# Stick-breaking attention on one core: the values product in plain fp32, two heads side by side on TensorE's columns

## The chip, the core and the metric

The kernel runs on one core of one Trainium2 chip. The metric is device microseconds for one execution of the whole program, of which the runs give a median and a lowest and highest. A profile of one execution gives the span, from the first to the last instruction, and the times of every instruction. The engines are called PE (TensorE's matmuls), PEld (its weight loads), DVE (VectorE), ACT (ScalarE), POOL (GpSimd) and SP (SyncE, which starts most transfers here).

## What is computed

A two-layer trunk over 512 tokens of width 1024. Layer 0 mixes tokens by stick-breaking attention with 16 heads of width 64; layer 1 mixes them by a gated MLP. Each is followed by a SwiGLU feed-forward part. Only the attention is touched:

```python
for qb in range(S // SB_QBLOCK):          # 4 blocks of 128 queries
    z = einsum('bhtd,bhsd->bhts', q[..., q0:kend, :], k[..., :kend, :]) * scale
    log_beta = log_sigmoid(z)
    log_1m = where(before, log_sigmoid(-z), 0.0)
    later = cumsum(log_1m, reverse=True) - log_1m
    a = where(before, exp(log_beta + later), 0.0)
    out = einsum('bhts,bhsd->bhtd', a, v[..., :kend, :])
```

The weights `a` of one head are a 512 x 512 triangle of 128 x 128 blocks, ten of them not empty. The last line, weights times V, is what this document calls the values product.

## The kernel before, in words

**Products of split numbers.** Nearly every product is made of reduced fp32 numbers (type F32R). A number is split (`split`, line 89) into a high part, which ACT writes (line 93), and a low part, the rest, which DVE subtracts (line 94). `mm3` (line 81) then issues three matmuls into one accumulator: high by high, high by low, low by high.

**The attention's stages** (lines 655 to 875). The sixteen heads go by pairs, a pair being 128 rows of q, k or 128 columns of V.

- V (lines 551 to 570) is computed first, in two halves of 512 columns; `v_evac` splits each half into `Vh` and `Vl`, four ACT copies and four DVE subtractions per half. They live in slots of the pool `s4`, which has 28.
- `scores` (line 738) multiplies q and k for some blocks of a pair. A head uses 64 of the array's 128 rows, and the two heads are issued in turn into two PSUM banks `zb`. ACT takes the sigmoid (line 759), DVE runs a scan (line 764) and a difference (line 769), which leaves the weights in `ga`.
- `flip` (line 775) turns three or four 128 x 128 blocks of weights on PE (line 78) into the bank `tw` of that head, and splits them into the tile `ar`, high and low part side by side; `ar` has two buffers.
- `values` (line 789) takes the turned blocks as the moving operand and V as the stationary one. For each head it goes over two pieces; a piece is one block row of V by 128 or 256 columns, and takes the three matmuls of `mm3`. All 128 columns of the pair's V are loaded for either head, so each of the two banks `av` has 64 rows of use and 64 rows that nobody reads.
- `finish` (line 804) copies the useful half of each `av` bank into one tile `of` (two ACT copies, line 810) and splits that into `o`, which the output projection reads later.

**Order of the work.** In the attention PE's order is written out by hand: `pe["chain"]` ties every matmul to the one before it. Per pair there are three flips of either head, three calls of `scores` for the next pair, and three calls of `values` per head (`LATE`, `EARLY[0]`, `EARLY[1]`). Between them `fill` issues steps of other products: q and k of later pairs (bank `pqk`, lines 676 to 685), and in the end parts of the output projection (bank `y`). One step of q and k is three matmuls of 512 columns. The piece widths of one head are 128 and 256 for `LATE` and for `EARLY[0]`, and 256 and 256 for `EARLY[1]`.

A background job `Bg` (line 274) computes the modulation vectors meanwhile: SP loads 512 KB tiles `rawada`, DVE multiplies and adds them (line 268, `G`, `A`, `B`). DVE and ACT also split the weights that PE will need (`wh`, `wl`, lines 93 and 94). The order on DVE and ACT is made by the scheduler when the program is built, not by hand; it follows the program's order roughly. DVE works its queue in order.

Of the kernel before, what the change touches and what calls it, by code (L numbers as in the profile page):

```python
# [8 lines left out]
F32 = mybir.dt.float32  # L9
F32R = mybir.dt.float32r  # L10
AF = mybir.ActivationFunctionType
ALU = mybir.AluOpType

P = 128
T = 512
# [10 lines left out]
def trunk(ctx: ExitStack, tc: tile.TileContext, A: dict, out: bass.AP):  # L26
# [6 lines left out]
    npool = ctx.enter_context(tc.tile_pool(name="npool", bufs=2))  # L33
# [9 lines left out]
    def nm(s):  # L43
        uid[0] += 1
        return f"{s}_{uid[0]}"

    def slot(dt, name, a=2, b=512):
        return s4.tile([P, a, b], dt, tag="s4", name=nm(name))

    def bank(name, tag="b"):  # L50
        return psum.tile([P, 512], F32, tag=tag, bufs=6 if tag == "b" else 2, name=nm(name))

    dve, act = nc.vector, nc.scalar
    pe = {"prev": None, "chain": False}

    def pe_op(b):

        if pe["chain"] and pe["prev"] is not None:
            order(b, pe["prev"])
        pe["prev"] = b  # L60

    def order(b, before):
        tc.add_manual_dep(
            b.ins, before.ins.name,
            mybir.DependencyInfo(mybir.DependencyClass.NoSync, mybir.DependencyReason.DATA),
            reason="order",
        )

    def mm(o, l, r, start, stop, after=None):
        b = nc.tensor.matmul(o, l, r, start=start, stop=stop, skip_group_check=True)  # L70
        pe_op(b)
        if after is not None:
            order(b, after)
# [3 lines left out]
    def transpose(o, i):  # L77
        last_tp[0] = nc.tensor.transpose(o, i, ident)  # L78
        pe_op(last_tp[0])

    def mm3(o, lh, ll, rh, rl, start, stop):
        mm(o, lh, rh, start, False)
        mm(o, lh, rl, False, False)
        mm(o, ll, rh, False, stop)
# [4 lines left out]
    def split(hi, lo, src, hi_dve=False):  # L89
        if hi_dve:  # L90
            dve.tensor_copy(hi, src)
        else:
            act.activation(hi, src, AF.Copy)  # L93
        dve.tensor_tensor(lo, src, hi.bitcast(F32), ALU.subtract)  # L94
# [453 lines left out]

    hT = new_hT()

    Vh = [[slot(F32R, "Vh") for _ in range(2)] for _ in range(2)]
    Vl = [[slot(F32R, "Vl") for _ in range(2)] for _ in range(2)]

    def v_step(vb, hf, k, w):
        for part in range(2):
# [11 lines left out]

    def v_evac(vb, hf):
        for tt in range(NT):
            split(Vh[hf][tt // 2][:, tt % 2, :], Vl[hf][tt // 2][:, tt % 2, :], vb[tt][:])  # L570

    onec = oneb[:, 0:1]

# [8 lines left out]
    def cols0(acc, n):  # L582

        ps = bank("ab0", "p")
        for i in range(n):
            mm(ps[:, i : i + 1], acc[:, i * P : (i + 1) * P], onec, True, True)
        return ps
# [31 lines left out]
    vb = [bank("v0") for _ in range(NT)]  # L619
# [7 lines left out]
    for b in range(1, 4):  # L627
# [7 lines left out]
        ps = cols0(acc, 4)  # L635
# [16 lines left out]
    fwork["raw"] = ctx.enter_context(tc.tile_pool(name="wraw2", bufs=2))  # L652
    v_evac(vb, 0)
    o8 = []
    with tc.tile_pool(name="att", bufs=1) as att, tc.tile_pool(name="att2", bufs=2) as att2:

        qk = {}

# [48 lines left out]
        def fill(n, at=None):  # L707
            for j in range(n):
                next(fgen, None)
                if j == at:  # L710
                    bg.step(1)
# [9 lines left out]
        def attend(i):  # L721

            weights = {}
            vc = slice(i % 4 * P, (i % 4 + 1) * P)
            vhf = i // 4

            def layout(js):
                offs, N = {}, 0
                for j in js:
                    offs[j] = N
                    N += T - P * j
                return offs, N

            def scores(js):

                q, kt = qk[i]  # L740
                offs, N = layout(js)
                for j in js:
                    o, n = offs[j], T - P * j
                    js_ = slice(j * P, (j + 1) * P)
                    for t, (a, b) in enumerate(((0, 0), (0, 1), (1, 0))):
                        for h in range(2):
                            r = slice(64 * h, 64 * h + 64)
                            mm(
                                zb[h][:, o : o + n], q[r, a, js_], kt[r, b, j * P : T],
                                j == js[0] and t == 0, t == 2,  # L750
                            )
                wide = js[0] != 2
                g = att.tile(
                    [P, 2, T + 4 if wide else 260], F32, tag=f"ga{wide}",
                    bufs=3 if wide else 1, name=nm("ga"),
                )
                with tc.issue_after(table.ins):
                    for h in range(2):
                        last_act[0] = act.activation(g[:, h, :N], zb[h][:, :N], AF.Sigmoid, scale=-1.0)

                for h in range(2):
                    for e, j in enumerate(js):
                        o, n = offs[j], T - P * j
                        dve.tensor_tensor_scan(  # L764
                            left[:, h, o + 1 : o + e + 1 + n], g[:, h, o - e : o + n],
                            tri[:, 1 - e : n + 1], 1.0, ALU.mult, ALU.max,
                        )
                M = N + len(js) - 1
                dve.tensor_tensor(g[:, :, :M], left[:, :, :M], left[:, :, 1 : M + 1], ALU.subtract)
                for e, j in enumerate(js):  # L770
                    weights[j] = (g, offs[j] + e)

            turned = {}

            def flip(blocks, h):

                ps = tw[h]
                n = 0
                for jj, js in blocks:
                    for j in js:  # L780
                        g, o = weights[j]
                        o += (jj - j) * P
                        transpose(ps[:, n : n + P], g[:, h, o : o + P])
                        n += P
                ar = att2.tile([P, 2, T], F32R, tag="ar", name=nm("ar"))
                split(ar[:, 0, :n], ar[:, 1, :n], ps[:, :n])
                turned[blocks[0][0], h] = ar

            def values(blocks, h, stop):

                ar = turned[blocks[0][0], h]
                start = blocks is LATE
                n = 0
                for jj, js in blocks:
                    w = len(js) * P
                    mm3(
                        av[h][:, js[0] * P : js[0] * P + w],
                        Vh[vhf][jj // 2][:, jj % 2, vc], Vl[vhf][jj // 2][:, jj % 2, vc],
                        ar[:, 0, n : n + w], ar[:, 1, n : n + w],
                        start and n == 0, stop and jj == 3,  # L800
                    )
                    n += w

            def finish():
                o = slot(F32R, "o")
                o8.append(o)
                f = npool.tile([P, 512], F32, tag="n", name=nm("of"))
                for h in range(2):
                    r = slice(64 * h, 64 * h + 64)
                    act.activation(f[r, :], av[h][r, :], AF.Copy)  # L810
                split(o[:, 0, :], o[:, 1, :], f[:])

            return scores, flip, values, finish

# [6 lines left out]
        LATE = ((2, (2,)), (3, (2, 3)))  # L821
        EARLY = ((0, (0,)), (1, (0, 1))), ((2, (0, 1)), (3, (0, 1)))
        vb = [bank("v1") for _ in range(NT)]
# [9 lines left out]
            bg.step(1)  # L833
        v_evac(vb, 1)
        tw = [bank("tw") for _ in range(2)]
        av = [bank("av") for _ in range(2)]
        fill(3, 1)
        cur[0](B0)
        for n in FIRST:
# [1 line left out]
        for i in range(NPAIR):  # L841
            scores, flip, values, finish = cur
            more = i + 1 < NPAIR
            F = iter(FILLS if i < 6 else LAST[i - 6])
            flip(LATE, 0)
            flip(LATE, 1)
            fill(next(F))
            if more:
                cur = attend(i + 1)
                cur[0](B31)  # L850
            fill(next(F), 1)
            values(LATE, 0, False)
            values(LATE, 1, False)
            fill(next(F))
            flip(EARLY[0], 0)
            flip(EARLY[0], 1)
            fill(next(F), 1)
            if more:
                cur[0](B2)
            fill(next(F), 1)  # L860
            values(EARLY[0], 0, False)
            values(EARLY[0], 1, False)
            flip(EARLY[1], 0)
            flip(EARLY[1], 1)
            fill(next(F))
            if more:
                cur[0](B0)
            fill(next(F), 1)
            values(EARLY[1], 0, True)
            values(EARLY[1], 1, True)  # L870
            finish()
        for _ in fgen:
            pass
# [361 lines left out]
```

## Time and profile before

| | before |
|---|---|
| time, median of 3 runs | 1181.23 us |
| lowest and highest | 1174.74 and 1182.79 us |
| span of the profiled execution | 1176.5 us |
| PE, PEld busy | 97%, 86% of the span |
| DVE, ACT busy | 75%, 47% of the span |
| mean granted TensorE clock | 0.990 |
| matmuls of the values product (`av`) | 288, from 112.0 to 268.4 us |

For the profiled execution the span is what is given; its own time is not listed apart from the three runs. The three runs lie within 0.7% of each other.

How to read it: a matmul's recorded time contains the way through the array, and matmuls overlap, so a sum of recorded times is more than the time that they take. What one matmul costs in a row of them is the distance from its start to the next start. In a timeline, the first column is the start, the second the time from the first start to the last end of a merged group, and brackets give idle time of the engine before it and who ended it. In the table of windows each engine has its busy time and, in brackets, the count of its instructions.

### The profile page before, as it was taken

Reading aid. Unit: us, or ns where it says so; the run is one execution under the profiler, and the core shown is the slowest. Engines: PE = TensorE matmul, PEld = TensorE weight load, DVE = VectorE, ACT = ScalarE, POOL = GpSimd, SP = SyncE. Lnnn points to the kernel's source line nnn. Section 1 sums busy time; section 2 is a strip of 40 time slices with the busy share of each in tenths; the row PEclk is TensorE's granted clock in tenths of the full one; section 3 lists DMA queues with packets and bytes.
Section 4 is the critical chain, followed back from the end, with each engine's and each line's share of the span. In section 5 each row is a group of like instructions: output and inputs, shape, how many; then the busy total and the mean of one; then the engine's idle time right before and its main releaser. Section 6 shows DMA issues by size and latency. Waiting matters only on the chain.

```text
span 1176.5 us, 18192 instructions
## 1 busy us (share of the span) xinstructions
PE 1140.3 (97%) x7296; PEld 1011.7 (86%) x7296; DVE 884.8 (75%) x1171; ACT 557.8 (47%) x935; POOL 20.2 (2%) x35
## 2 busy tenths in 40 slices
PE   5999999999999999999999999999999999999997
PEld 4776778888999999998878887988999999988886
DVE  6888998875998988878686864668889898873213
ACT  6444444554665555563143633526555555572112
POOL 0100000000000000000000100001000000000000
PEclk8999999999999999999999999999999999999999
DMA  8666452113424444338886473324244544244211
GB/s 328 201 213 231 144 161 72 55 54 126 160 92 144 134 139 142 122 112 262 281 286 237 151 250 125 109 71 156 80 143 126 161 127 142 75 127 160 90 54 72
DMA packets 48777, 173.93 MB, mean 148 GB/s; under 512 B 5674, under 2 KB 6058, under 8 KB 48692
## 3 DMA queue, kind: packets, MB, share of 16 engines
q1 hardware_dynamic: 46964, 166.48, 43.7%
q0 software_dynamic: 1728, 6.29, 1.4%
q8 instruction: 57, 0.93, 0.3%
q14 instruction: 28, 0.23, 0.1%
HBM read 164.36 MB, written 8.39 MB: 147 GB/s over the span
## 4 chain that ended last, share of the span: by engine, by line
PE 73%; DVE 11%; DMA 10%; ACT 3%; issue 3%; SPq 0%; DVEq 0%; ACTq 0%
PE r L70 31%; PE y L70 20%; DMA rawada<-in_ada 5%; PE v L70 4%; PE pqk L70 4%; PE gu L70 4%; DVE wl L94 2%; PE av L70 2%; PE u L70 2%; DVE left L764 1%; PE z L70 1%; DVE B L268 1%; DMA raw<-in_wdown 1%; PE tw L78 1%; DMA raw<-in_win_v 1%
## 5 line engine op out<-in xcount | busy, mean ns | idle before, releaser
L70 PE MATMUL y<-wh,as 128*128 128x512 f32 x832 | 264.0, 395 | 0.4 <-ACT gu L964 0.4
L93 ACT ACTIVATE wh<-raw 128x1024 fp32r<-128x1024 f32 x112 | 118.3, 1060 | 215.4 <-PE y L70 102.7
L94 DVE TENSOR_TENSOR wl<-raw,wh 128x1024 fp32r<-128x1024 f32 x112 | 136.3, 1221 | 107.4 <-ACT wh L93 107.1
L70 PEld LDWEIGHTS y<-wh,as 128*128 128x128 f32 x832 | 156.2, 188 | 37.4 <-ACT gu L964 0.8
L70 PE MATMUL r<-Sh,wl 128*128 128x256 f32 x608 | 170.3, 280 | 0.0
L70 PE MATMUL r<-Sh,wh 128*128 128x256 f32 x608 | 170.0, 280 | 0.0
L70 PE MATMUL r<-Sl,wh 128*128 128x256 f32 x608 | 170.0, 280 | 0.0
L70 PE MATMUL y<-wl,as 128*128 128x512 f32 x416 | 164.4, 395 | 0.0
L94 DVE TENSOR_TENSOR wl<-f,wh 128x1024 fp32r<-128x1024 f32 x76 | 92.8, 1221 | 36.4 <-ACT wh L93 36.4
L70 PEld LDWEIGHTS r<-Sh,wh 128*128 128x128 f32 x608 | 114.7, 189 | 0.0
L93 ACT ACTIVATE wh<-f 128x1024 fp32r<-128x1024 f32 x76 | 80.7, 1061 | 71.4 <-PE r L70 64.9
L70 PEld LDWEIGHTS r<-Sl,wh 128*128 128x128 f32 x608 | 114.5, 188 | 0.0
L70 PEld LDWEIGHTS r<-Sh,wl 128*128 128x128 f32 x608 | 114.5, 188 | 0.0
L70 PEld LDWEIGHTS y<-wl,as 128*128 128x128 f32 x416 | 78.2, 188 | 18.0
L70 PE MATMUL r<-hTh,wh 128*128 128x256 f32 x304 | 89.0, 293 | 0.0
L70 PE MATMUL r<-hTl,wh 128*128 128x256 f32 x304 | 84.9, 280 | 0.0
L70 PE MATMUL r<-hTh,wl 128*128 128x256 f32 x304 | 80.2, 280 | 0.0
L70 PEld LDWEIGHTS r<-hTh,wh 128*128 128x128 f32 x304 | 57.2, 188 | 5.4 <-DVE gu L959 1.0
L70 PE MATMUL r<-hTh,b 128*128 128x256 f32 x304 | 60.7, 282 | 0.0
L70 PE MATMUL v<-wh,hTh 128*128 128x512 f32 x128 | 53.2, 416 | 6.0 <-ACT hTh L599 6.0
L70 PEld LDWEIGHTS r<-hTl,wh 128*128 128x128 f32 x304 | 57.4, 189 | 0.1
L93 ACT ACTIVATE wh<-rawx 128x1024 fp32r<-128x1024 f32 x38 | 40.4, 1063 | 35.2 <-PE r L70 30.9
(203 smaller groups left out, 2530.4 us busy)
## 6 DMA issues: line engine op xcount, KB each, us to landing
rawada<-in_ada SPq DMA_DIRECT2D x80, 512.0 KB, 4.5
raw<-in_wdown SPq DMA_DIRECT2D x44, 512.0 KB, 4.1
rawy<-in_wy SPq DMA_DIRECT2D x38, 512.0 KB, 3.7
rawx<-in_wx SPq DMA_DIRECT2D x38, 512.0 KB, 4.6
raw<-in_wqk SPq DMA_DIRECT2D x16, 512.0 KB, 4.8
ada<-in_ada0p SPq DMA_DIRECT2D x12, 512.0 KB, 8.2
raw<-in_wgu SPq DMA_DIRECT2D x12, 512.0 KB, 4.0
xd<-x POOLq DMA_DIRECT2D x12, 512.0 KB, 2.9
```

What stands on the lines that cost most here:

```text
L70: b = nc.tensor.matmul(o, l, r, start=start, stop=stop, skip_group_check=True)
L78: last_tp[0] = nc.tensor.transpose(o, i, ident)
L93: act.activation(hi, src, AF.Copy)
L94: dve.tensor_tensor(lo, src, hi.bitcast(F32), ALU.subtract)
L268: dve.scalar_tensor_tensor(acc, w, sc[:, kk : kk + 1], acc, ALU.mult, ALU.add)
L764: dve.tensor_tensor_scan(left[:, h, o + 1 : o + e + 1 + n], g[:, h, o - e : o + n], tri[:, 1 - e : n + 1], 1.0, ALU.mult, ALU.max,)
```

## The change

What it does, part by part:

1. V is kept as one plain fp32 tile per slot, copied from PSUM by ACT. `Vl` and its DVE subtractions are gone, and four slots of `s4` with them.
2. The turned weights `ar` are one plain fp32 tile, copied by ACT. Their low part and the DVE subtraction are gone; the tile is half as large and has four buffers in place of two.
3. `values` takes both heads of a pair in one call. For each piece it issues one plain fp32 matmul per head: 64 columns of V as the stationary operand, and the result in rows 0 to 63 or 64 to 127 of one bank, so that the two heads take the two halves of the array's columns.
4. The two banks are now used in turn by pairs (`avs[i % 2]`), not one per head.
5. `finish` splits the bank directly. The tile `of` and its two ACT copies are gone.

The order of calls on PE stays as it was, with a pair of `values` calls become one.

```diff
-    Vh = [[slot(F32R, "Vh") for _ in range(2)] for _ in range(2)]
-    Vl = [[slot(F32R, "Vl") for _ in range(2)] for _ in range(2)]
+    V = [[slot(F32, "V") for _ in range(2)] for _ in range(2)]
...
-            split(Vh[hf][tt // 2][:, tt % 2, :], Vl[hf][tt // 2][:, tt % 2, :], vb[tt][:])
+            act.activation(V[hf][tt // 2][:, tt % 2, :], vb[tt][:], AF.Copy)
...
-    with tc.tile_pool(name="att", bufs=1) as att, tc.tile_pool(name="att2", bufs=2) as att2:
+    with tc.tile_pool(name="att", bufs=1) as att, tc.tile_pool(name="att2", bufs=4) as att2:
...
-                ar = att2.tile([P, 2, T], F32R, tag="ar", name=nm("ar"))
-                split(ar[:, 0, :n], ar[:, 1, :n], ps[:, :n])
+                ar = att2.tile([P, T], F32, tag="ar", name=nm("ar"))
+                act.activation(ar[:, :n], ps[:, :n], AF.Copy)
...
-            def values(blocks, h, stop):
-
-                ar = turned[blocks[0][0], h]
+            def values(blocks, stop):
+
                 start = blocks is LATE
                 n = 0
                 for jj, js in blocks:
                     w = len(js) * P
-                    mm3(
-                        av[h][:, js[0] * P : js[0] * P + w],
-                        Vh[vhf][jj // 2][:, jj % 2, vc], Vl[vhf][jj // 2][:, jj % 2, vc],
-                        ar[:, 0, n : n + w], ar[:, 1, n : n + w],
-                        start and n == 0, stop and jj == 3,
-                    )
+                    for h in range(2):
+                        lane = slice(64 * h, 64 * h + 64)
+                        mm(
+                            avs[i % 2][lane, js[0] * P : js[0] * P + w],
+                            V[vhf][jj // 2][:, jj % 2, vc][:, lane],
+                            turned[blocks[0][0], h][:, n : n + w],
+                            start and n == 0, stop and jj == 3,
+                        )
                     n += w
...
-                f = npool.tile([P, 512], F32, tag="n", name=nm("of"))
-                for h in range(2):
-                    r = slice(64 * h, 64 * h + 64)
-                    act.activation(f[r, :], av[h][r, :], AF.Copy)
-                split(o[:, 0, :], o[:, 1, :], f[:])
+                split(o[:, 0, :], o[:, 1, :], avs[i % 2][:])
...
-        av = [bank("av") for _ in range(2)]
+        avs = [bank("av") for _ in range(2)]
...
-            values(LATE, 0, False)
-            values(LATE, 1, False)
+            values(LATE, False)
...
-            values(EARLY[0], 0, False)
-            values(EARLY[0], 1, False)
+            values(EARLY[0], False)
...
-            values(EARLY[1], 0, True)
-            values(EARLY[1], 1, True)
+            values(EARLY[1], True)
```

## The prediction, made before the changed kernel ran

> **What bounds the kernel now.** I read the busy times first, then the busy times by stretch, then the waits of PE inside the attention.
>
> ```profile
> PE 1140.3 (97%) x7296; PEld 1011.7 (86%) x7296; DVE 884.8 (75%) x1171; ACT 557.8 (47%) x935; POOL 20.2 (2%) x35
> ```
> ```profile
> 57.00:100.00 43.00, 42.68 (x194) 33.07 (x193) 34.77 (x41) 20.65 (x31) 2.17 (x3) 1.00 0.68 228
> 100.00:122.00 22.00, 17.31 (x96) 13.35 (x95) 20.60 (x25) 6.47 (x12) 0.00 (x0) 0.99 0.67 215
> 122.00:275.00 153.00, 150.46 (x918) 123.17 (x917) 125.39 (x167) 77.55 (x140) 0.00 (x0) 0.99 0.28 87
> 275.00:320.00 45.00, 44.34 (x270) 38.69 (x270) 36.51 (x51) 26.23 (x54) 3.23 (x5) 1.00 0.51 175
> ```
> ```profile
> PE z L70 <- DVE k L94: 2.4, 2, 2.0
> PE pqk L70 <- DVE q L662: 2.3, 1, 2.3
> PE av L70 <- DVE ar L94: 2.3, 2, 1.9
> PE v L70 <- ACT hTh L599: 0.3, 1, 0.3
> PE y L70 <- DVE k L94: 0.2, 1, 0.2
> ```
>
> PE is busy for 97% of the span, so time is won or lost by what PE streams, by what it pays between streams, and by its few waits. The stretches (columns PE, PEld, DVE, ACT, POOL) say where the waits are: from 100 to 122 us DVE is busy for 20.60 of 22 us while PE has only 17.31. Everywhere else around the attention PE is nearly full. The waits from 57 to 275 us come to 7.5 us, and 7.2 of that ends with a DVE operation. So there are three sums to make: the stream of the values product, the changes of TensorE's layout, and those waits.
>
> **The stream as it is.** The chain of waits shows whole calls of `values`, both heads, twelve matmuls each; the three below are one round of `EARLY[1]`, `LATE` and `EARLY[0]`. The timeline shows one `EARLY[1]` pair of calls.
>
> ```profile
> 174.03 1.42 PE av L70 x12
> ...
> 180.87 1.38 PE av L70 x12
> ...
> 188.30 1.38 PE av L70 x12
> ```
> ```profile
> 129.78 0.40 PE L70 MATMUL av<-ar,Vh 128*128 128x256 f32 x2
> ...
> 131.07 0.28 PE L70 MATMUL av<-ar,Vl 128*128 128x256 f32 x1
> 131.19 0.82 PE L78 MATMUL tw<-identt,ga 128*128 128x128 f32 x6
> 131.77 0.48 PE L70 MATMUL pqk<-hTh,wh 128*128 128x512 f32 x1
> ```
>
> Twelve matmuls of 256 columns take 131.19 - 129.78 = 1.41 us, so 0.1175 each. A `LATE` call has six of 256 and six of 128; 1.38 - 6 x 0.1175 leaves 0.112 for one of 128 columns. Half the columns save almost nothing: a floor of 0.11 us. Per pair of heads 1.42 + 1.38 + 1.38 = 4.18 us, in eight pairs 33.4 us. This goes.
>
> **The stream that comes.** Per piece and head one plain product takes the place of three. The kernel has plain fp32 products already, with one column, in the start-up:
>
> ```profile
> L70 PEld LDWEIGHTS ab<-oneb,acc x32: 186/192/192, 17.8 to 56.0; 128*128 128x128 f32 x32
> L70 PE MATMUL ab<-oneb,acc x32: 165/250/271, 17.8 to 56.1; 128*128 128x1 f32 x32
> ```
>
> `cols0` issues 2 + 2 + 4 + 4 + 4 = 16 products, and there are 32 loads and 32 matmuls: one plain product is two loads and two matmuls. So the new `values` has 12 products per pair of heads, 24 records, 192 in all, against 288. What a record costs with 128 or 256 columns no row shows. Its lower bound is the reduced matmul above, 0.1175 us for 256 columns. The kernel splits numbers by hand because one pass carries a reduced number; if a record loads one part of V, it still has to pass the high and the low part of the moving operand, twice the columns. Then 256 columns cost what 512 cost, and 128 what 256 cost. The rows for 512 stand here, with a visit of `scores` between them:
>
> ```profile
> 132.77 0.39 PE L70 MATMUL pqk<-hTl,wh 128*128 128x512 f32 x1
> 133.01 0.40 PE L70 MATMUL pqk<-hTh,wl 128*128 128x512 f32 x1
> 133.33 1.13 PE L70 MATMUL z<-k,q 64*128 64x128 f32 x12
> 134.39 0.50 PE L70 MATMUL pqk<-hTh,wh 128*128 128x512 f32 x1
> 134.73 0.40 PE L70 MATMUL pqk<-hTl,wh 128*128 128x512 f32 x1
> 134.97 0.39 PE L70 MATMUL pqk<-hTh,wl 128*128 128x512 f32 x1
> ```
>
> 134.97 - 134.73 and 133.01 - 132.77 give 0.235 us. I take 0.235 for a record of 256 columns and 0.1175 for one of 128. The upper bound is twice that again, if a record makes all four combinations.
>
> The Trainium skill, FP8 and Floating Point Precision, Matmul Precision, says that true fp32 takes four passes through the array; over two records that is the two passes each that I take, and no run here shows it with more than one column.
>
> Next, whether the two halves work at once. For rows, the trace says yes. The twelve `z` matmuls are six pairs, three of 128 and three of 384 columns. One after the other they would need 6 x 0.112 + 6 x 0.175 (midway between 256 and 512) = 1.72 us; they are through in 1.06 us (133.33 to 134.39) with all that surrounds them. For columns no row exists; `z` is the nearest, and I take overlap. But the order is not that of `scores`, which alternates heads matmul by matmul. Here head 0 issues both its records, then head 1. Two records on one half cannot overlap each other, and matmuls start in program order, so only neighbours of different heads overlap: head 0's second record with head 1's first, head 1's second with head 0's first of the next piece. Four products, eight records, take five steps. `EARLY[1]`: 5 x 0.235 = 1.17 us. `LATE` and `EARLY[0]`: 2 x 0.1175 + 3 x 0.235 = 0.94 us. Per pair of heads 3.05 us, in eight 24.4 us: 9.0 less than before. Bounds: complete overlap, four steps, 2 x (0.1175 + 0.235) = 0.71 and 0.94, in eight pairs 18.9 us (14.5 less); no overlap, eight steps, 1.41 and 1.88, in eight pairs 37.6 us (4.2 more).
>
> **The changes of layout.** The new calls address half the columns, where the old ones took the whole array. A visit of `z` shows what leaving the whole array costs: from 133.01 to 134.73 are 1.72 us. Two matmuls of 512 take 0.47, six pairs at their own rate 3 x 0.112 + 3 x 0.175 = 0.86, so 0.39 us is paid for going in and out; 0.105 of it is visible in the step after the visit, 134.73 - 134.39 = 0.34 against 0.235. Bounds: nothing, if columns need no such change, and 0.39. I take 0.35, near the row, since the loads are half as wide. There are 24 calls, each between matmuls on the whole array: 24 x 0.35 = 8.4 us.
>
> The Trainium skill's TensorEngine Tiling (Array Packing), Key Properties, says that changing the tiling mode drains TensorE while changing the tile does not. The `z` visit agrees with 0.39 us; by the rule a column call pays the same, 24 x 0.39 = 9.4 us.
>
> **The waits.** DVE loses these operations, ACT the fourth row:
>
> ```profile
> L94 DVE TENSOR_TENSOR ar<-tw,ar 128x384 fp32r<-128x384 f32 x32 | 16.8, 550 | 3.7 <-ACT ar L93 3.7
> L94 DVE TENSOR_TENSOR ar<-tw,ar 128x512 fp32r<-128x512 f32 x16 | 10.4, 686 | 6.2 <-ACT ar L93 6.2
> L94 DVE TENSOR_TENSOR Vl<-v,Vh 128x512 fp32r<-128x512 f32 x8 | 5.0, 683 | 3.0 <-ACT Vh L93 3.0
> L810 ACT ACTIVATE of<-av 64x512 f32<-64x512 f32 x16 | 9.5, 594 | 2.6 <-PE av L70 1.3
> ```
>
> 32.2 us off DVE and 9.5 off ACT, worth what PE waited for. The copies of V and `ar` on ACT stay, at the same shapes. The clearest wait is this one, and behind it is a second loss:
>
> ```profile
> 119.20 0.22 PE L70 MATMUL av<-ar,Vh 128*128 128x128 f32 x1
> 121.33 0.33 PE L70 MATMUL av<-ar,Vh 128*128 128x128 f32 x1 [1.91 <-DVE ar L94]
> ```
> ```profile
> 116.47 0.86 ACT L93 ACTIVATE ar<-tw 128x384 fp32r<-128x384 f32 x2
> 120.73 1.01 DVE L94 TENSOR_TENSOR ar<-tw,ar 128x384 fp32r<-128x384 f32 x2
> ```
> ```profile
> 121.33 2.38 PE av L70 x11
> 123.71 1.64 PE tw L78 x8
> ```
>
> ACT had both tiles at 117.33, DVE came to them at 120.73. Without the subtraction PE goes on at 119.20: 1.9 us. After that pause PE runs slow: eleven matmuls take 2.38 us, against twelve in 1.38, and eight transposes 1.64, against 0.58 for six (from 131.19 to 131.77 above, so 0.8 for eight). That is 1.8 us, and it goes if the pause goes. The other 0.4 of `av` waits goes for the same reason. The 2.3 us for `q` and 2.4 + 0.2 for `k` are DVE being late; DVE had spent 2.48 us on four `Vl` and 1.28 us on two `ar` in front of these:
>
> ```profile
> 93.57 2.48 DVE L94 TENSOR_TENSOR Vl<-v,Vh 128x512 fp32r<-128x512 f32 x4
> ...
> 104.60 0.69 DVE L662 SCALAR_TENSOR_TENSOR q<-pqk,q 128x512 fp32r<-128x512 f32 x1
> 105.99 1.28 DVE L268 SCALAR_TENSOR_TENSOR A<-rawada,sc,A 128x1024 f32<-128x1024 f32 x1 [0.71 <-DMA rawada<-in_ada]
> ```
>
> Late next are the `rawada` transfers: the last row's DVE waited 0.71 us for one, and nothing behind it in the queue passes. So I don't take all of the 4.9 us but 3. Together 1.9 + 1.8 + 0.4 + 3 = 7 us less. Bounds: 9.0 (all of it) and 0 (every pause comes back for another operation).
>
> **The rest at nothing.** `finish` becomes one ACT rounding and one DVE subtraction from PSUM, without the two copies; its result is read by the output projection, after other matmuls, and no wait for `o` stands among PE's. The bank change frees `av` earlier, and no wait for it exists either. Four buffers of half the size take the same space, and a flip's copy already follows its transposes. Four free slots may make the scheduler put operations on DVE and ACT in another order: 3 us either way, in the range. No transfer, and nothing on SP or POOL, is added, removed or moved.
>
> **Sum.** -9.0 + 8.4 - 7 = -7.6 us. The profiled span of 1176.5 us becomes 1168.9. The median lies 4.7 us above that span, and I lay the difference on the median: 1181.2 - 7.6 = 1173.6 us.
>
> **Rivals.**
> - Column halves cost less than row halves: no price for the change, staggered overlap: -9.0 - 7 = -16, so 1165 us; with complete overlap 1160. For it: nothing of the row operand changes between calls. Against: the `z` visit pays each time.
> - No overlap of columns: +4.2 + 8.4 - 7 = +5.6, so 1187 us. For it: both halves need all 128 rows of two different moving streams at once, where the halves of `z` share the 128 rows out. Against: DVE's relief, which gives most of it back.
> - Slower: a load for one half can't run under the stream of the other, and each record shows its load. Its price is the 0.105 us seen after the `z` visit: 192 x 0.105 = 20 us, and with no overlap either, +4.2 + 8.4 + 20 - 7 = +26, so 1207 us. With staggered streams it is +12.6 (1194). It decides from about 0.1 us a record; below 0.04 the kernel is not slower. Records that make four passes end there as well: 37.6 more by the serial bound, some 24 more staggered. Against it: in `z`, loads do run under streams.
> - The waits return as waits for `rawada`: -9.0 + 8.4 = -0.6, so 1180.6 us. It lies in the forecast's own range.
>
> **Chances.** Forecast, staggered overlap with a paid change: 0.42, its own range 1166 to 1181. Cheap change: 0.18. No overlap: 0.20. Exposed loads or more passes: 0.20. The range to hold 8 in 10 reaches from the cheap change with complete overlap to the staggered case with exposed loads and some more: 1160 to 1198. A measurement of this kernel can tell about 1%, 11.8 us, from no change. Faster by more: most of the cheap change and a little of the forecast, 0.21. Slower by more: nearly all of the last, 0.20. Within 1%: 0.59.
>
> **What would show it.** Right: 192 `av` records; starts some 0.235 us apart for 256 columns with two of them together; calls near 1.2 to 1.5 us with both changes; a step of about 0.34 after each call; no `av` wait at 119 us, and full speed after it. Wrong: records 0.47 us apart, a call over 1.9 us, or a new wait of PE on ACT's `ar` copies.

## The result and the profile after

The changed kernel takes 1164.96 us (median of 4 runs, 1164.09 to 1167.9), the kernel before beside it 1179.38 us. The ratio of the changed kernel to the one before is 0.9897, with a 95% interval of 0.9870 to 0.9923: 12 us less, between 9 and 15. A second comparison, on another occasion (run e8 below), gave 0.9913 (0.9890 to 0.9936), 10 us less. The prediction said 7.6 us less, with 1160 to 1198 us as its range: the direction is right, the size is too small, and the terms of the sum were further off than the sum.

The profiled execution took 1164.45 us, its span 1162.3 us against 1176.5 before. These are the page's busy times of the changed kernel, and three of the stretches shown for the kernel before (the columns are PE, PEld, DVE, ACT, POOL, granted clock, DMA share, GB/s):

```profile
PE 1128.7 (97%) x7200; PEld 982.5 (85%) x7200; DVE 856.1 (74%) x1115; ACT 548.1 (47%) x919; POOL 20.2 (2%) x35
```
```profile
57.00:100.00 43.00, 43.00 (x196) 33.59 (x196) 34.25 (x36) 19.24 (x29) 0.78 (x1) 1.00 0.67 232
100.00:122.00 22.00, 20.46 (x110) 14.52 (x109) 17.50 (x19) 7.68 (x15) 0.00 (x0) 0.92 0.74 240
122.00:275.00 153.00, 149.31 (x846) 104.78 (x845) 104.40 (x125) 70.50 (x129) 0.00 (x0) 0.99 0.31 95
```

PE has 96 records less, 288 old ones against 192 new. DVE has lost 28.7 us. Between 100 and 122 us PE is now busy for 20.46 us where it had 17.31; part of that is slow running, since the granted clock there is 0.92.

Not all of the 14 us of span are the change's. The first matmul behind the last `av` record starts at 258.15 us, before at 268.51, which is 10.4 us earlier. Of these, 1.3 us were there by 40 us, ahead of all that the change touches: from 36.5 to 39.5 us the granted clock was 0.50 in the execution of the kernel before and 1.00 in that of the changed one. That leaves 9.1 us for the attention. The other 3.8 us lie behind it, where the work is the same: the execution of the kernel before has two more stretches at 0.50 there (716 to 719 and 832 to 835 us), the one of the changed kernel none. Such stretches come and go between executions. The changed kernel profiled again (e8 below) has the early one, and the kernel before with one edit (e11) has neither of the late ones. So these 5 us are not put down to the change.

The waits of PE in the attention (from 57 to 275 us):

```profile
PE z L70 <- DVE k L94: 4.7, 2, 3.2
PE y L70 <- DVE k L94: 0.4, 1, 0.4
```

The waits for `q` and `ar` have gone, as predicted. But what PE waits for `k` has grown from 2.4 to 4.7 us, and one of the two waits is longer than any before. In all 7.5 us of waits have become 5.1.

The values product, first its records, then a `LATE` and an `EARLY[1]` call in the timeline of PE. A merged row carries the shape of its first member, and its second column runs to the end of its last one.

```profile
L70 PEld LDWEIGHTS av<-ar,V x192: 132/136/137, 110.9 to 257.1; 128*64 128x64 f32 x192
L70 PE MATMUL av<-ar,V x192: 272/379/431, 110.9 to 257.3; 128*64 128x256 f32 x128, 128*64 128x128 f32 x64
```
```profile
130.22 0.40 PE L70 MATMUL pqk<-hTh,wl 128*128 128x512 f32 x1
130.55 0.87 PE L70 MATMUL av<-ar,V 128*64 128x128 f32 x8
131.35 0.50 PE L70 MATMUL pqk<-hTh,wh 128*128 128x512 f32 x1
131.68 0.39 PE L70 MATMUL pqk<-hTl,wh 128*128 128x512 f32 x1
...
143.26 0.39 PE L70 MATMUL pqk<-hTh,wl 128*128 128x512 f32 x1
143.58 1.08 PE L70 MATMUL av<-ar,V 128*64 128x256 f32 x8
144.60 0.88 PE L78 MATMUL tw<-identt,ga 128*128 128x128 f32 x6
145.23 0.48 PE L70 MATMUL pqk<-hTh,wh 128*128 128x512 f32 x1
```

The `LATE` call with all it costs: from 130.22 to 131.68 are 1.46 us; two matmuls of 512 take 0.47, so 0.99 against 1.38 before. `EARLY[1]`: 143.26 to 144.60 less 0.235, and 0.05 more for the six transposes behind it (0.63 against 0.58), is 1.16 against 1.42. `EARLY[0]` is as long as `LATE` in its first part and as `EARLY[1]` behind it: 0.95 against 1.38. Per pair of heads 3.10 against 4.18 us, in eight pairs 8.6 us less on PE's own path.

Where the other part should have come from, the waits, is the place to look at next. DVE and PE of the changed kernel, around the longest wait:

```profile
140.07 1.28 DVE L268 SCALAR_TENSOR_TENSOR B<-rawada,sc,B 128x1024 f32<-128x1024 f32 x1
143.88 1.28 DVE L268 SCALAR_TENSOR_TENSOR B<-rawada,sc,B 128x1024 f32<-128x1024 f32 x1 [2.53 <-DMA rawada<-in_ada]
145.08 2.34 DVE L763 TENSOR_TENSOR_SCAN left<-ga,tri 128x512 f32<-128x512 f32 x2
147.33 1.20 DVE L94 TENSOR_TENSOR wl<-raw,wh 128x1024 fp32r<-128x1024 f32 x1
148.45 1.22 DVE L768 TENSOR_TENSOR ga<-left 128x1024 f32<-128x1024 f32 x1
149.59 0.69 DVE L94 TENSOR_TENSOR k<-pqk,k 128x512 fp32r<-128x512 f32 x1
```
```profile
150.33 1.02 PE L70 MATMUL z<-k,q 64*128 64x128 f32 x10 [3.19 <-DVE k L94]
151.27 0.79 PE L70 MATMUL pqk<-hTh,wh 128*128 128x512 f32 x1
151.87 0.63 PE L70 MATMUL pqk<-hTl,wh 128*128 128x512 f32 x1
152.29 0.63 PE L70 MATMUL pqk<-hTh,wl 128*128 128x512 f32 x1
```

DVE stands idle for 2.53 us until a background tile has landed. In all it waits 6.5 us for `rawada` between 57 and 275 us, where it waited 3.2 us before. Behind that sit the scan, a weight split, a difference, and then `k`, for which PE waits 3.19 us. And after that pause PE runs slow: the first matmul of 512 columns takes 151.87 - 151.27 = 0.60 us, where a first one takes 0.34 elsewhere, and the next takes 152.29 - 151.87 = 0.42 us, not 0.235. The same happens behind the other wait for `k`, 1.54 us long, which ends at 106 us. The granted clock (the third number from the end) shows both stretches, and the one that stood behind the wait for `ar` in the kernel before; first the row of the kernel before, then those of the changed one:

```profile
122.00:125.00 3.00, 3.00 (x17) 3.00 (x16) 2.70 (x4) 0.40 (x1) 0.00 (x0) 0.50 0.54 197
```
```profile
107.00:110.00 3.00, 3.00 (x10) 2.21 (x8) 2.57 (x3) 1.09 (x2) 0.00 (x0) 0.50 0.83 244
151.50:154.50 3.00, 3.00 (x8) 2.32 (x9) 2.96 (x5) 0.95 (x2) 0.00 (x0) 0.50 0.48 124
```

By the starts of the matmuls, each of the three costs some 1.5 us. So where the kernel before has one slow stretch in the attention, the changed kernel has two.

### The profile page after: what moved, and what is told of

The parts are those of the page before. It is cut to its first block, busy times and chain, and to the rows that moved or that the text cites. A ratio compares the mean times of both kernels' runs of the same rounds, so it can differ in the third digit from the quotient of the medians.

```text
span 1162.3 us, 17935 instructions
## 1 busy us (share of the span) xinstructions
PE 1128.7 (97%) x7200; PEld 982.5 (85%) x7200; DVE 856.1 (74%) x1115; ACT 548.1 (47%) x919; POOL 20.2 (2%) x35
## 4 chain that ended last, share of the span: by engine, by line
PE 73%; DVE 11%; DMA 10%; issue 3%; ACT 3%; SPq 0%; DVEq 0%; ACTq 0%
PE r L70 32%; PE y L70 20%; DMA rawada<-in_ada 6%; PE pqk L70 5%; PE gu L70 4%; PE v L70 3%; DVE wl L94 2%; PE u L70 2%; PE z L70 1%; PE av L70 1%; DVE left L763 1%; DMA raw<-in_wdown 1%; PE tw L78 1%; DVE B L268 1%; PE sv L70 1%
## 5 line engine op out<-in xcount | busy, mean ns | idle before, releaser
L763 DVE TENSOR_TENSOR_SCAN left<-ga,tri 128x128 f32<-128x128 f32 (+2 forms) x64 | 48.4, 810 | 24.1 <-ACT ga L758 24.1
```

Source lines behind the costliest of these rows:

```text
L763: dve.tensor_tensor_scan(left[:, h, o + 1 : o + e + 1 + n], g[:, h, o - e : o + n], tri[:, 1 - e : n + 1], 1.0, ALU.mult, ALU.max,)
```

## The experiments

The theory after reading the two traces: the two halves of the columns work fully at once, which wins some 16 us of stream and pays 7 for the layout; DVE's relief is worth little, since a transfer takes its place as what is late. The rivals: DVE's relief makes the gain and the stream does not matter; or the halved products are simply cheap, overlap or not. The runs came in three groups, each beside runs of the kernel before: e1 to e4, then e5 to e8, then e9 to e12.

**e1: the heads apart.** A call issues both pieces of head 0, then both of head 1.

```diff
-                for jj, js in blocks:
-                    w = len(js) * P
-                    for h in range(2):
+                for h in range(2):
+                    n = 0
+                    for jj, js in blocks:
+                        w = len(js) * P
...
```

> The changed kernel, but a call of values issues both pieces of head 0 and then both pieces of head 1, so that neighbouring products use the same half of the columns. Theory (the gain is that the two halves work at once): only one record per call, at the seam between the heads, can still overlap. A LATE or EARLY[0] call grows from 0.65 to about 1.19 us of streaming, EARLY[1] from 0.86 to 1.50, so 1.7 us per pair of heads and some 14 us in all: about 1179 us against 1165. Rival (the gain is DVE's relief, the stream does not matter): no change, 1165. Third possibility (PE takes matmuls of the other half ahead of those that wait for their own): between the two, 1165 to 1172.

Measured: 1166.5 us, ratio 0.9915 (0.9898 to 0.9931), as the changed kernel. The timeline:

```profile
132.63 0.40 PE L70 MATMUL pqk<-hTh,wl 128*128 128x512 f32 x1
132.96 0.88 PE L70 MATMUL av<-ar,V 128*64 128x128 f32 x8
133.77 0.50 PE L70 MATMUL pqk<-hTh,wh 128*128 128x512 f32 x1
...
146.01 1.09 PE L70 MATMUL av<-ar,V 128*64 128x256 f32 x8
```

A call is as long as before the edit (0.88 and 1.09 against 0.87 and 1.08). In the trace the records come in twos, 6 to 7 ns apart in the changed kernel and 13 to 14 ns apart here. The theory's number of 1179 us fell. Its rival's 1165 came in, but so did the third possibility's 1165 to 1172, and the rival's reason is not thereby right. Two explanations are left: PE starts the work of one half ahead of earlier work that waits for the other half, or no overlap takes place at all and a halved product is cheap. The next run separates them.

**e5: one half only.** Both heads use columns 0 to 63, each with its own bank; layout changes stay, and nothing can work at once.

```diff
-                            avs[i % 2][lane, js[0] * P : js[0] * P + w],
+                            avs[h][0:64, js[0] * P : js[0] * P + w],
...
-                split(o[:, 0, :], o[:, 1, :], avs[i % 2][:])
+                f = npool.tile([P, 512], F32, tag="n", name=nm("of"))
+                for h in range(2):
+                    act.activation(f[64 * h : 64 * h + 64, :], avs[h][0:64, :], AF.Copy)
+                split(o[:, 0, :], o[:, 1, :], f[:])
```

> The changed kernel, but both heads of a pair use the first half of the columns and each its own bank; finish copies the two useful halves together. Layout changes stay, and no two products can work at once. Theory (the halves work at once, whatever the order of issue): the stream goes from 17.3 to 34.3 us over the eight pairs, 17 us more than the changed kernel, so the ratio to the kernel before is about 1.004. Rival (no overlap is needed, a halved product is simply cheap): the ratio of the changed kernel, 0.99.

Measured: 1179.0 us, ratio 1.0019 (1.0003 to 1.0034), against 0.9913 (0.9890 to 0.9936) of the changed kernel in the same group (**e8**, no edit, 1166.8 us):

> The changed kernel without any edit, timed beside the next three on one chip. All theories: the ratio of the first comparison again, 0.987 to 0.992. It is there to compare the others with.

```profile
130.15 0.40 PE L70 MATMUL pqk<-hTh,wl 128*128 128x512 f32 x1
130.48 1.51 PE L70 MATMUL av<-ar,V 128*64 128x128 f32 x8
131.92 0.50 PE L70 MATMUL pqk<-hTh,wh 128*128 128x512 f32 x1
...
144.41 0.39 PE L70 MATMUL pqk<-hTh,wl 128*128 128x512 f32 x1
144.73 1.94 PE L70 MATMUL av<-ar,V 128*64 128x256 f32 x8
146.60 0.87 PE L78 MATMUL tw<-identt,ga 128*128 128x128 f32 x6
```

Here eight records of 256 columns start one after another: (1.94 - 0.38) / 7 = 0.22 us apart (0.38 is the median record). In the changed kernel first and last start lie 1.08 - 0.38 = 0.70 us apart, three such steps: eight records start in four twos. So the overlap is complete, and with e1 it does not hang on the order of issue. A call is 1.77 - 1.13 = 0.64 us longer here for `LATE` and `EARLY[0]`, and 2.19 - 1.34 = 0.85 for `EARLY[1]`: 17.0 us in eight pairs, the theory's number. (The two ACT copies in `finish` are back as well, but PE waits for neither a bank nor `o` here.) The time rose by only 12. A slower PE waits less for DVE: the waits for `k` were 3.4 us here and 5.6 in e8, and no slow stretch followed them, where e8 has two in the attention. That is the first sign that what the stream wins is partly given back in those waits.

**e2: plain fp32 on whole columns.** The products take all 128 columns, each head its own bank, `finish` as in the kernel before.

```diff
-                            avs[i % 2][lane, js[0] * P : js[0] * P + w],
-                            V[vhf][jj // 2][:, jj % 2, vc][:, lane],
+                            avs[h][:, js[0] * P : js[0] * P + w],
+                            V[vhf][jj // 2][:, jj % 2, vc],
...
```

> Plain fp32 as in the changed kernel, but each head's product takes all 128 columns of V and has its own bank, as in the kernel before; finish copies the two useful halves again. No change of layout, no overlap, DVE relieved of the low parts. Theory: records of 128 and 256 columns at 0.11 and 0.213 us one after the other make 34.3 us over the eight pairs against 17.3, and 7.6 us of layout changes go: +9.4, so about 1174 us; what is then still missing to 1179 is worth of DVE's relief, 2 to 6 us. Rival (relief makes the gain): 1165. If overlap and relief were both worth nothing: 1179.

Measured: 1170.5 us, ratio 0.9954 (0.9939 to 0.9969), 5.4 us less than the kernel before.

```profile
131.10 0.39 PE L70 MATMUL pqk<-hTh,wl 128*128 128x512 f32 x1
131.33 1.47 PE L70 MATMUL av<-ar,V 128*128 128x128 f32 x8
132.45 0.58 PE L70 MATMUL pqk<-hTh,wh 128*128 128x512 f32 x1
```

Plain fp32 by itself wins nothing on PE: four records of 128 and four of 256 columns one after another, with the product behind them, take about what twelve reduced ones took. By the starts in the traces they take 1.4 us more over all calls. So the halves are what wins on PE's path. The 5.4 us, and this 1.4, must come from elsewhere; the waits of PE fell from 7.5 to 4.8 us, which is less than half of it. The granted clock was 0.992 to 0.994 in its runs and 0.990 to 0.993 in those of the kernel before, worth some 2 us. The rest no run explains. In the two profiled executions the attention of e2 is only 2.3 us shorter than before; 5 us of their difference lie behind it, where the kernel before has its two late slow stretches and e2 has none.

**e3 and e6: DVE's work put back, in two ways.** In e3 DVE computes the low parts of V and of the turned weights again, into tiles that nobody reads. In e6 DVE and not ACT makes the copies of the turned weights, so that PE's `av` matmuls hang on DVE's queue again.

```diff
...
+                lo = att2.tile([P, T], F32, tag="lo", bufs=2, name=nm("lo"))
+                dve.tensor_tensor(lo[:, :n], ps[:, :n], ar[:, :n], ALU.subtract)
```
```diff
-                act.activation(ar[:, :n], ps[:, :n], AF.Copy)
+                dve.tensor_copy(ar[:, :n], ps[:, :n])
```

> The changed kernel with DVE's 56 subtractions put back: they write the low parts of V and of the turned weights into tiles that nobody reads, so DVE has the 32 us of work again and PE's stream is that of the changed kernel. Theory: only the relief is lost, 2 to 6 us: 1167 to 1171. Rival (the gain is DVE's relief): 1177 to 1180, as the kernel before. If the relief is worth nothing: 1165.

> The changed kernel with the copies of the turned weights moved from ACT to DVE: DVE has about the work of the old subtractions again and PE's values wait for DVE again, not only for ACT. Theory A (the relief is that values no longer depend on DVE's late queue): waits of av on DVE of 2 to 4 us come back, with a slow stretch of the clock behind the longest, 3 to 6 us more than the changed kernel. Theory B (the relief is DVE's load, or nothing): 0 to 2 us more, as with the load alone put back.

Measured: e3 1165.2 us, ratio 0.9911 (0.9891 to 0.9930); e6 1164.8 us, ratio 0.9891 (0.9869 to 0.9914). Neither differs from the changed kernel. The waits of PE in e3 and then in e6:

```profile
PE z L70 <- DVE k L94: 4.1, 3, 2.9
PE pqk L70 <- DVE q L665: 1.9, 1, 1.9
PE tw L78 <- DVE lo L791: 1.1, 1, 1.1
PE y L70 <- DVE k L94: 0.4, 1, 0.4
```
```profile
PE z L70 <- DVE k L94: 3.9, 2, 2.4
PE y L70 <- DVE k L94: 0.4, 1, 0.4
```

With the load back, waits of PE come back, for `q` among them, and make 7.5 us in all; yet the time stays. In e6 no wait for `ar` came back at all, so it says nothing of what such a wait would cost. The relief of DVE by 32 us is therefore worth nothing that these runs can tell, some 4 us at most. The rival that DVE's relief makes the gain is out.

**e4 and e7: one visit per pair.** The three calls of `values` stand together at the place of the last, with six `ar` buffers.

```diff
...
-            values(LATE, False)
...
-            values(EARLY[0], False)
...
+            values(LATE, False)
+            values(EARLY[0], False)
             values(EARLY[1], True)
```

In e4 the values of `LATE` read the turned weights of `EARLY[1]`; in e7 each call reads its own.

> The changed kernel with the three calls of values of a pair moved together to the place of the last, so that TensorE goes to the halved columns 8 times and not 24 (six buffers of turned weights in place of four). Theory (each visit pays about 0.31 us for going in and out): 16 x 0.31 = 5.0 us less, 1160. Rival (a visit costs nothing by itself, the time is the stream's): 1165. If the later values hold up something behind them: more than 1165.

> The three calls of values of a pair together at the place of the last, with the turned weights of each call kept apart. Theory (a visit to the halved columns costs 0.31 us): 16 x 0.31 = 5.0 us less than the changed kernel on PE's path; the first build of this, whose values of LATE read the weights of EARLY[1] in place of their own, was 11 us below the changed kernel's first runs, of which 2.5 us was a shorter wait for k and 1.7 us a slow stretch less. So 6 to 11 us less, a ratio of 0.980 to 0.985. Rival (the time came from the wrong tile being read): the ratio of the changed kernel.

Measured: e4 1153.6 us, ratio 0.9815 (0.9800 to 0.9829); e7 1154.9 us, ratio 0.9799 (0.9772 to 0.9825). So 11 to 12 us less than the changed kernel, where the layout alone explains 5. The row of one visit in e7:

```profile
158.13 0.39 PE L70 MATMUL pqk<-hTh,wl 128*128 128x512 f32 x1
158.46 2.38 PE L70 MATMUL av<-ar,V 128*64 128x128 f32 x24
160.77 0.87 PE L78 MATMUL tw<-identt,ga 128*128 128x128 f32 x6
```

Three calls in 2.64 us (158.13 to 160.77), where the three take 1.13 + 1.13 + 1.34 = 3.60 us in the changed kernel. Less the two 512-column steps that the removed places still take (0.47) and with the 0.10 and 0.05 that a first matmul after each of them cost, it is 0.64 us a pair, 5.1 in all: the theory's number for 16 visits. The rest is not in the calls. What the profiled executions show is fewer waits and slow stretches. That of e4, at 1153.8 us, has 2.2 us of waits in place of 5.1, and one slow stretch in the attention in place of two. That of e7 has 2.0 us of waits, no slow stretch and a granted clock of 0.996, but at 1147.8 us it is 6 us faster than any other execution of e7, so the others need not look like it. When `values` is moved, the order on DVE and the time at which `k` is wanted move as well, and no run holds these fixed.

**e9 and e11: a third buffer for the background tiles.** In the attention `rawada` has three buffers in place of two, in the changed kernel (e9) and in the one before (e11).

```diff
-                        raw = fwork["raw"].tile([P, D], F32, tag="raw2", name=nm("rawada"))[:]
+                        third = k % 3 == 2 and "third" in fwork
+                        pool, tag = (fwork["third"], "raw3") if third else (fwork["raw"], "raw2")
+                        raw = pool.tile([P, D], F32, tag=tag, name=nm("rawada"))[:]
...
```

> The changed kernel with a third buffer for the background tiles rawada during the attention. Theory (PE's faster stream is partly given back: DVE waits 2.5 us for one rawada transfer at 141 us, with k's subtraction behind it in its queue, and PE waits 3.2 us for k and then runs through a slow stretch of the clock): with the transfer started earlier that wait of DVE goes, PE's waits for k fall from 5 to at most 2 us, and 3 to 6 us go in all, a ratio to the kernel before of 0.986 to 0.989 against 0.991. Rival (DVE is late by its own load): the waits stay, 0.991.

> The kernel before with the third buffer for rawada. Theory (before the change it was DVE's load and not the transfer that was late: 1.4 + 0.7 us of DVE waits on rawada against 7.2 us of PE waits on DVE): 0 to 2 us less, ratio 0.998 to 1.0. Rival (the transfer was always what was late): 3 to 6 us less, 0.995 to 0.997, and then the third buffer has nothing to do with the change.

Measured: e9 1159.9 us, ratio 0.9863 (0.9846 to 0.9879), by the ratios 4 to 6 us less than the changed kernel. e11 1172.8 us, ratio 0.9968 (0.9953 to 0.9983), 4 us less. DVE of e9 at the place of the wait, and PE's longest waits in e9 and then in e11:

```profile
138.30 3.92 DVE L268 SCALAR_TENSOR_TENSOR B<-rawada,sc,B 128x1024 f32<-128x1024 f32 x3
142.13 2.34 DVE L766 TENSOR_TENSOR_SCAN left<-ga,tri 128x512 f32<-128x512 f32 x2
```
```profile
PE z L70 <- DVE k L94: 2.3, 2, 2.0
```
```profile
PE av L70 <- DVE ar L94: 2.3, 3, 1.0
PE z L70 <- DVE k L94: 1.6, 2, 1.2
```

The three background steps now run without a gap, DVE's wait for `rawada` falls from 6.5 to 1.4 us, the waits of `z` for `k` halve, and one of the two slow stretches is gone. The theory holds for the changed kernel. For the one before, the rival's number came in: the transfer was late there too. DVE's wait for `rawada` falls from 3.2 to 0.4 us, and PE's waits fall from 7.5 to 4.4 us. So the third buffer is no part of what the change did; it takes away a brake that both have. Between e11 and e9 the change is worth 1 - 0.9863 / 0.9968 = 1.1%, 12 us.

**e10 and e12: together.** e10 has one visit per pair and the third buffer; e12 has the visit right behind the pair's last `scores`, before the fill.

> One visit to the halved columns per pair, and the third buffer for rawada as well. If the two edits are independent: 1155 us less what is left of the waits for k, 2 us, so about 1153 (ratio 0.978 to 0.980). If the third buffer only moves the wait elsewhere: 0.980 as without it.

> As the kernel with one visit and the third buffer, but the visit to the halved columns stands right behind the pair's last scores, which use the halved rows, with no matmul on the whole array between them. Theory A (each change of layout drains the array, and one drain between the two layouts takes the place of two): 0.2 to 0.3 us less in each of 7 pairs, 1 to 2 us in all, 0.977 to 0.979. Theory B (halved rows to halved columns costs twice a single change): no gain. If the values come before the copies of the turned weights are there, a wait of PE on ACT shows and takes it back.

Measured: e10 1151.4 us, ratio 0.9777 (0.9754 to 0.9800), the fastest here and faster than both kernels; e12 1152.0 us, ratio 0.9804 (0.9779 to 0.9829). In e12 the array goes from halved rows to halved columns at once:

```profile
159.14 0.96 PE L70 MATMUL z<-k,q 64*128 64x512 f32 x6
160.03 2.38 PE L70 MATMUL av<-ar,V 128*64 128x128 f32 x24
162.35 0.50 PE L70 MATMUL pqk<-hTh,wh 128*128 128x512 f32 x1
```

The visit is as long as in e7. By the starts in the traces, going directly saves 0.15 us a pair, 1 us in all, and PE's wait for `k` was 2.5 us in e12 against 1.3 in e10: nothing is left that the measurement could show. Theory A holds in the rows and not in the time.

## Why the prediction was too small

**The stream (predicted 9.0 us less).** It was 16 less. In the working, the step that failed is "matmuls start in program order, so only neighbours of different heads overlap". e1 and e5 showed in its place that work for one half of the columns starts while earlier work waits for the other half, and that eight records need four steps, not five. This was the prediction's bound for complete overlap (14.5 less, at 0.235 us for a record of 256 columns); the record itself is 0.215 to 0.22, which adds to it: 4 x 0.215 = 0.86 us for `EARLY[1]`, 2 x 0.11 + 2 x 0.215 = 0.65 for the others, 17.3 us in eight pairs against 33.4.

**What a record costs.** The choice of two passes a record was right. The bounds of 0.1175 and 0.47 us for 256 columns are both excluded by e5, where 0.22 stands alone. The Trainium skill's FP8 and Floating Point Precision, Matmul Precision, says that true fp32 takes four passes. The trace agrees, with 0.44 us a product of 256 columns against 0.1175 for a reduced one.

**The layout (predicted 8.4 us more).** What the three calls cost beyond their stream is 0.99 - 0.65, 0.95 - 0.65 and 1.16 - 0.86: 0.34, 0.30 and 0.30 us, 7.5 us over 24 visits. e7 took 16 of them out and won 5.1 us on PE's path. This term was right, at 0.31 us a visit and not the 0.39 of a `z` visit. The Trainium skill's TensorEngine Tiling (Array Packing), Key Properties, says that a change of tiling mode drains TensorE. The trace agrees in that a visit to halved columns is paid each time, as one to halved rows is; that the 0.31 us are a drain, no row shows.

**The waits (predicted 7 less, bounds 0 and 9).** The wait for `ar` went as told, with the slow stretch behind it, and so did the wait for `q`. But the waits fell by 2.4 us only, from 7.5 to 5.1, and with two slow stretches for one some 1.5 us came on top, so this term is 0.9 less in all. The step that failed is the choice of 3 of the 4.9 us by which DVE was late, and that it counted a slow stretch that goes and none that comes. "Late next are the `rawada` transfers" was right, and was under-weighed: this term went nearly the way of the rival in which the waits return as waits for `rawada`. e3 and e6 say that the relief itself is worth nothing measurable, e9 that the transfer is what holds.

**The sum.** -16.1 + 7.5 - 2.4 + 1.5 = -9.5 us. The attention of the two profiled executions differs by 9.1 us, and the two ratios say 12 and 10, with intervals that reach from 7.5 to 15. The two misses had opposite signs, 7 us too little from the stream and 6 too much from the waits. That they nearly cancel is luck, and it is why the forecast came near. What is not settled is e2, whose 6.8 us beside the stream its waits and its clock explain by two thirds, and e7, where some 6 us lie outside the calls.

**The rivals.** The measured 1165 us lies just below the forecast's own range, 1166 to 1181, and on the number of the first rival, a change of layout that costs nothing. That rival's mechanism did not occur: each visit costs 0.31 us, and e7 wins back what 16 visits cost. Exposed loads did not occur either: with one half only, the eight records of e5 start 0.22 us apart, the time of their columns. "No overlap" is what e5 does. The prediction priced it at 5.6 us more than the kernel before; measured are 0.2% more, 2 us. The stream was priced too high there: it is 17.3 + 17.0 = 34.3 us, 0.9 more than before and not 4.2, since a record costs 0.215 us and not 0.235. With 7.5 for the layout, 4.1 less for the waits (7.5 to 3.4) and 1.5 less for the one slow stretch that is gone, the rows give 2.8 us more.

## What to carry to other kernels

Two products with 64 output columns each can share the array, and cost one product's time whatever their order of issue; what one pays is about 0.3 us for each visit, so gather the visits. When an engine that is the bound gets faster, look at which transfer or queue was just in time before: here a third buffer for an unrelated background load was worth 4 to 6 us, about half as much as the whole change. And put two terms of opposite sign to the test one by one: a sum that comes out near says little about its terms.

## What the runs showed of the hardware

- A plain fp32 product is two loads and two matmuls. Each matmul takes about as long as one of twice its columns in reduced fp32: 0.22 us at 256 columns, where 512 reduced ones take 0.235, and 0.11 us at 128, where 256 reduced ones take 0.1175.
- The two column halves are not bound to program order between them: in e1 the second head's first record starts 13 to 14 ns after the first head's, although both pieces of the first head were issued before it.
- A load of 64 columns is recorded at 136 ns, one of 128 at 188 ns.
- After a pause of PE matmuls can run at about half speed for some 3 us (6 in e8), with a granted clock of 0.50: 0.42 us in place of 0.235 for 512 columns at 152 us. It happened behind pauses of 1.54 and 3.19 us in the changed kernel and of 1.91 us in the kernel before, and not behind pauses of 2.33 and 1.99 us in the kernel before or 2.05 us in e7. So the length of the pause alone did not decide it here.
